# Attention of an encoder layer on one core: two more heads turned by VectorE's blocks and a trip through DRAM, eight weights' low parts by adding transfer, and a new order

## The chip, the core and the metric

The program runs on one core of a Trainium2 chip. The core has TensorE (in the profile PE for matmuls and PEld for weight loads), VectorE (DVE), ScalarE (ACT), GpSimd (POOL) and SyncE (SP, which here only issues transfers). Each engine works through its own queue in order; semaphores hold an instruction until what it needs is there. The metric is the device time of one execution in microseconds (us), here the median of three runs.

## The reference, cut to what matters

One layer for 512 tokens of width 1024, all in float32: a half-step feed-forward network, a mixing stage, a second half-step feed-forward network, a last norm.

```python
x = x + 0.5 * swiglu(rms_norm(x, ffn1_norm), ffn1_w_gate, ffn1_w_up, ffn1_w_down)
h = rms_norm(x, mix_norm)
u = h @ w_in                                   # 1024 -> 512 + 512 + 128 + 128
f_out = fourier_mixer(u[..., :512], fnet_w, fnet_b)
a_out = gqa_attention(u[..., 512:1024], u[..., 1024:1152], u[..., 1152:], q_norm, k_norm)
x = x + jnp.concatenate([f_out, a_out], axis=-1) @ w_out
x = x + 0.5 * swiglu(rms_norm(x, ffn2_norm), ffn2_w_gate, ffn2_w_up, ffn2_w_down)
return rms_norm(x, final_norm)
```

The attention has 8 query heads of 64 channels and 2 key and value heads. For every head the scores are 512 by 512; a softmax runs over the keys; the probabilities then multiply the values.

## The kernel before, in words

Every large matrix product is made of three products of two parts: a value is split into a high part (rounded to the type that the profile calls fp32r) and a low part (the value less its high part). ScalarE makes a high part with a cast, VectorE a low part with a subtraction (`lows`, L204).

The change lies in the mixing stage, lines 850 to 1480. There the program is written as some 630 small named operations, and the string `ORDER` lists their names: each engine gets the instructions of the operations in the order of this list, SyncE's and GpSimd's transfers too. Outside the mixing stage `ORDERS` fixes VectorE's and ScalarE's order; it isn't changed.

The names that are needed:

- `k.0` to `k.7`, `q0.0` to `q3.7`, `v.0` to `v.7`: steps of three matmuls (128 by 512) of the projections. `wq3`, `wv`, `f0` to `f3`, `fw`, `o0` to `o7` are weights of 512 KB (fw half): `.r` loads one into a buffer called raw, `.h` makes its high part (L917), `.l` its low part. There are three raw buffers; one comes free when `.h` and `.l` have read it.
- The four pairs t = 0 to 3 hold the query heads (t, 0) and (t, 1). c counts blocks of 128 queries, kc blocks of 128 keys. `s`tc makes the scores of both heads in two PSUM banks (L1294), `m`tc the negative maxima (VectorE), `e`tbc the exponentials (ScalarE, L1320), which write the tile th of the head, `g`tc the inverse sums, `n`tbc the scaling of th by them (ScalarE, L1356).
- The probabilities must then be turned, so that keys lie along the partitions. For six of the eight heads TensorE does it: `t`tbkc is four transposes of 128 by 128 into a PSUM bank (L1333), `h` and `l` split what it gives (L1338 on ScalarE, L204 on VectorE) into the tiles ph and pl.
- For heads 00 and 01 (`BY_BLOCKS`) it goes otherwise. `T`tbg turns the 32 by 32 blocks of 512 columns in place on VectorE (L1233). `Z`tbg writes these columns, 256 KB, to DRAM (SyncE, L1239). `z`tbg reads 256 KB back into 32 of the 128 partitions of the tile pt (L1246), so that four of them fill pt. `h` (L1260) and `l` split pt.
- `v`tbkc multiplies the values by the two parts (L1367). `o`tb`.c`, `.a` and `r`t bring a pair into place for the output projection.
- `f`hc, `d`, `c`, `map` are the Fourier mixer (L1097 to L1204). `y`d`.0` to `y`d`.7` are the output projection's 64 steps, three matmuls each (L260).

The tiles th and pt have two buffers each: the heads of pair 1 take over the buffers of pair 0.

`ORDER` sets the order of the work and nothing else.

Of the kernel before, what the change touches and what calls it, by code (L numbers as in the profile page):

```python
# [48 lines left out]

ORDERED = {getattr(mybir.EngineType, e) for e in ("PE", "DVE", "Activation", "Pool", "SP")}  # L50
ORDER = """
wk.r wk.h wq0.r wv.r wk.l k.0 k.1 k.2 wq1.r k.3 wq0.h k.4 k.5 k.6 k.7 wq0.l n1.c q0.0 wq2.r cos k.sq wq3.r k.pq q0.1
q0.2 k.sw q0.3 q0.4 n1.m f1.r f2.r q0.5 k.s0 q0.6 k.rc wq1.h wq1.l wq2.h q0.7 k.s1 kw kp q0.sw k.rs q1.0 q1.1 wq2.l
q1.2 km q0.rc q1.3 k.h q1.4 k.l q1.5 q0.sq q0.rs q0.pq q1.6 wv.h q0.s0 q2.0 q0.h q1.7 q0.s1 q0.l wv.l wq3.h s00 q1.sw
m00 s01 s02 m01 q2.1 q2.2 q2.3 q1.sq q1.sd m02 wq3.l e000 q2.4 e010 q2.5 s03 g00 q1.rc e001 q2.6 f0.r e011 q2.7 g01
e002 m03 e012 v.0 q1.pq n000 n011 n001 e013 q3.0 q3.1 q1.rs v.1 e003 g02 f0.h g03 f0.l n010 f3.r n002 q1.s0 n003 v.2
q1.h T002 v.3 q2.sw n013 q1.l T001 T003 q3.2 n012 T013 q3.3 v.4 v.5 q1.s1 n1.p q2.sd q2.sq v.6 q3.4 v.7 Z001 T010 Z003
Z002 q3.5 T000 q3.6 T012 vt s13 s10 Z013 Z012 T011 f1.h q2.rc m13 e103 s11 q3.7 Z000 m11 f1.l m10 q3.sw Z010 q3.sq
e113 f00.0 q2.rs Z011 q3.rc f02.0 f2.h g13 z013 z010 e111 f00.1 f03.0 f2.l vp e101 e110 q3.pq vs z011 e100 z012 s12
h011 h012 v.h m12 v.l z001 l011 h010 f02.1 z003 g10 f00.u e112 q2.pq f01.0 q3.sd e102 l010 f02.e n110 f10.0 n100 v010  # L60
v011 f3.h fw.r g11 z002 z000 n101 f03.1 q2.h q3.rs h013 q2.s0 h000 l012 f12.0 n103 g12 f3.l f01.1 l000 n113 q2.s1 n102
q3.s0 f01.u v012 f03.e h002 o5.r t101 v000 n111 l013 t100 h001 q2.l f10.1 fw.h f03.h f10.u v013 l001 l002 f12.1 v001
h003 v002 q3.h f03.l fw.l l003 f12.e t102 n112 h100 h101 l101 l100 o2.r v003 o01.c o00.c s22 s23 h102 o00.a o01.a v100
l102 v101 pos t103 m22 t110 r0.h f02.h f11.0 h103 m23 f11.1 h110 e212 f12.h f11.u t112 f02.l v102 l103 e213 l110 t113
t111 h112 e203 o0.r v103 q3.l l112 s21 g23 e202 s20 f13.0 o10.c f13.1 n203 m21 h113 e211 o10.a map1 e201 m20 o2.h l113
v110 e200 e210 o2.l d00 map1.h g21 f13.e o1.r map1.l n201 map0 h111 map0.h g22 d01 g20 d10 l111 d11 d0.h n202 d0.l
v111 v112 n200 d1.h f13.h t200 v113 c0.s map0.l f12.l d1.l h200 c1.c f13.l o11.c c0.c c1.s c0.q l200 q3.s1 c0.o t201
n210 o11.a d20 t202 n212 o3.r c1.q h201 d21 h202 c1.o n213 t203 d2.h v200 l201 l202 s33 h203 s32 d2.l n211 v201 l203
c2.s t212 c0.h o0.h m33 m32 d30 d31 e313 t211 h212 c2.q d3.h c0.l e312 v202 h211 l212 c2.c v203 t210 t213 d3.l c2.o
s31 l211 h210 l210 c3.s m31 v210 e302 o0.l c1.h v211 c3.q c1.l s30 m30 o1.h v212 e311 e303 e301 y0.0 c2.h o1.l o6.r  # L70
o4.r g31 g32 e310 h213 e300 l213 c2.l c3.c y0.1 g33 g30 y2.0 n301 n302 n303 y2.1 y1.0 y1.1 v213 r0.l y0.2 y2.2 y1.2
n300 t301 c3.o t300 o20.c t302 o20.a t303 c3.h n311 c3.l y1.3 h300 y0.3 h301 n313 l300 h302 v300 l302 l301 h303 n310
y1.4 y2.3 v301 n312 o21.c t310 o21.a h310 y2.4 t311 l310 t312 v302 t313 r1.h l303 r2.h v303 r1.l h311 v310 l311 v311
h312 h313 o30.c l312 y0.4 l313 v312 o30.a v313 r2.l o31.c y2.5 o31.a y0.5 y2.6 r3.h y1.5 r3.l y1.6 y2.7 o5.h y1.7 y0.6
o5.l y0.7 y0.x y5.0 y5.1 o3.h o7.r y5.2 o3.l y3.0 y2.x y2.h y5.3 y2.q y3.1 y1.x y3.2 y5.4 y3.3 y2.l y5.5 y5.6 o6.h
y5.7 y3.4 o4.h y1.h o4.l y3.5 y3.6 y3.7 y1.q y4.0 o6.l y0.q y5.x y4.1 y6.0 y3.x y6.1 y4.2 y4.3 y0.h o7.h y1.a y5.q
y6.2 y4.4 y4.5 y2.a y6.3 y3.q y4.6 y4.7 o7.l y4.x y5.h y3.a y6.4 y1.l y4.q y0.l y6.5 y4.a y3.h y6.6 y6.7 y5.l y7.0
y7.1 y6.x y7.2 y5.a y6.h y3.l y7.3 y6.l y6.q y7.4 y6.a y7.5 y4.h y7.6 y7.7 y7.x y4.l y7.q y7.a y7.h y7.l
"""


# [54 lines left out]
def asf(ap):  # L136
    return ap.bitcast(F32)
# [19 lines left out]
def encoder(ctx, tc, A, out):  # L157
    nc = tc.nc
# [21 lines left out]
    dp = ctx.enter_context(tc.tile_pool(name="outside", bufs=1, space=bass.MemoryType.DRAM))  # L180
# [584 lines left out]
    n0, n1 = Norm(0), Norm(1)  # L765
# [89 lines left out]
    with tc.tile_pool(name="mix", bufs=1) as mp, tc.tile_pool(name="mixt", bufs=1) as mt:  # L855
# [4 lines left out]
        pos = mp.tile([P, 4 * 258 + 3 * 256], F32R, name="pos")  # L860
# [9 lines left out]
        cos = mp.tile([P, S], F32, name="cos")  # L870
# [31 lines left out]
        raws, ws = {}, {}  # L902

        def weight_ops(name, src, n=KD):
            @op(f"{name}.r")
            def _():
                raws[name] = raw_tile(src, name, n)

            @op(f"{name}.h")
            def _():  # L910
                ws[name] = hi, lo = tuple(weight_slots())
                if name in FURTHER_IN:

# [3 lines left out]
                (nc.vector.tensor_copy if name in HI_DVE else nc.scalar.copy)(hi[:, :n, :], raws[name][:, :n, :])  # L917
# [105 lines left out]
        kw = tp.tile([P, 4, 2, HD], F32, tag="wide", bufs=1, name="kw")  # L1023
# [203 lines left out]
        def block_ops(t, b):  # L1227

            for g in range(4):

                @op(f"T{t}{b}{g}")
                def _(g=g):
                    nc.vector.transpose(heads[t, b][:, g], heads[t, b][:, g])  # L1233

                @op(f"Z{t}{b}{g}")
                def _(g=g):
                    if (t, b) not in outside:
                        outside[t, b] = dp.tile([4, P, S], F32, tag="blocks", bufs=4, name=f"out{t}{b}")
                    nc.sync.dma_start(out=outside[t, b][g], in_=heads[t, b][:, g])  # L1239

                @op(f"z{t}{b}{g}")
                def _(g=g):
                    if (t, b) not in moved:
                        moved[t, b] = mt.tile([P, 4, S], F32, tag="pt", bufs=2, name=f"pt{t}{b}")
                    source = outside[t, b][g].rearrange("(a i) f -> i a f", a=4)
                    nc.sync.dma_start(out=moved[t, b][g * 32 : (g + 1) * 32], in_=source)  # L1246

            def natural(p):
                return p.rearrange("p (c a j) -> p a c j", c=4, a=4)

            for kc in range(4):
                n = f"{t}{b}{kc}"

                def source(kc=kc):
                    return moved[t, b][:, :, kc * P : (kc + 1) * P].rearrange("p a (c j) -> p a c j", c=4)

                @op(f"h{n}")
                def _(n=n, source=source):
                    ph = mt.tile([P, S], F32R, tag="ph", bufs=3, name=f"ph{n}")
                    nc.scalar.copy(natural(ph), source())  # L1260
# [450 lines left out]
```

## Time and profile before

| | |
|---|---|
| time, median of 3 runs (lowest, highest) | 816.61 us (816.13, 816.92) |
| the profiled execution | 816.57 us, of which the span of the profile is 814.8 us |
| PE busy | 806.6 us, 99% |
| DVE busy, ACT busy, POOL busy | 648.6, 498.2, 66.6 us |
| granted TensorE clock | 0.998 |
| the mixing stage's matmuls | 330.22 to 482.77 us |

Times in the profile count from the span's start. A busy engine counts an instruction from its start to its end, overlapped parts once; a mean of one instruction counts them each time. Where the text gives a window such as 400 to 432, it is from a view that lists the busy time of each engine in a stretch.

### The profile page before, as it was taken

How to read it: one execution, taken by the hardware profiler on the slowest of the kernel's cores; microseconds unless marked ns; L12 is line 12 of the kernel's file. 1: busy time of each engine (PE TensorE's matmuls, PEld its weight loads, DVE VectorE, ACT ScalarE, POOL GpSimd, SP SyncE). 2: the span in 40 equal slices, each digit the busy share in tenths (PEclk: the TensorE clock that was granted, in tenths of full speed). 3: DMA queues.
4: the chain of work that ended last, by engine and by line, in shares of the span. 5: the costliest groups of instructions: out<-in, count | busy, mean ns of one | idle time of the engine just before them, and what ended most of it. 6: DMA issues, size and time to landing. Idle time of an engine off the chain costs nothing.

```text
span 814.8 us, 13024 instructions
## 1 busy us (share of the span) xinstructions
PE 806.6 (99%) x4936; PEld 721.5 (89%) x4936; DVE 648.6 (80%) x1065; ACT 498.2 (61%) x864; POOL 66.6 (8%) x75
## 2 busy tenths in 40 slices
PE   9999999999999999999999999999999999999997
PEld 6888998899989998888888888899988998899987
DVE  7997997489956867799998578999955997489674
ACT  7883674267623735687999549557633674267462
POOL 0320000000000000020200003100100000000001
PEclk9999999999999999999999999999999999999999
DMA  7884553345443423339301146554443553345223
GB/s 259 194 178 161 152 137 82 133 130 168 85 139 95 129 72 117 120 111 262 124 27 52 62 123 146 130 188 140 134 118 114 153 140 83 130 130 144 61 78 103
DMA packets 39838, 103.95 MB, mean 128 GB/s; under 512 B 4704, under 2 KB 10976, under 8 KB 39776
## 3 DMA queue, kind: packets, MB, share of 16 engines
q1 hardware_dynamic: 30080, 86.80, 32.9%
q0 software_dynamic: 8832, 15.34, 11.2%
q10 hardware_dynamic: 864, 0.98, 0.4%
q8 instruction: 38, 0.62, 0.3%
q14 instruction: 24, 0.20, 0.1%
HBM read 95.51 MB, written 4.19 MB: 122 GB/s over the span
## 4 chain that ended last, share of the span: by engine, by line
PE 92%; ACT 3%; DVE 3%; issue 1%; DMA 1%; POOL 0%; POOLq 0%; DVEq 0%
PE dn L260 26%; PE r L510 12%; PE r L515 8%; PE gu L260 8%; PE mix L260 6%; PE q L510 4%; PE q L515 4%; PE r L506 4%; PE p L506 4%; PE q L506 4%; PE gu L814 3%; PE p L515 2%; PE mix L1367 2%; PE mix L1333 1%; ACT th L1320 1%
## 5 line engine op out<-in xcount | busy, mean ns | idle before, releaser
L260 PE MATMUL dn<-at,ring 128*128 128x512 f32 x900 | 202.5, 380 | 0.0
L260 PEld LDWEIGHTS dn<-at,ring 128*128 128x128 f32 x900 | 168.0, 188 | 28.7
L515 PE MATMUL r<-rt,ring 128*128 128x256 f32 x560 | 154.3, 276 | 0.0
L510 PE MATMUL r<-rt,ring 128*128 128x256 f32 x840 | 147.0, 276 | 0.0
L510 PEld LDWEIGHTS r<-rt,ring 128*128 128x128 f32 x840 | 127.0, 188 | 1.6
L515 PEld LDWEIGHTS r<-rt,ring 128*128 128x128 f32 x560 | 105.1, 188 | 0.2
L465 ACT CAST ring<-s 128x1024 fp32r<-128x1024 f32 x70 | 73.6, 1051 | 35.5 <-PE r L510 16.5
L204 DVE TENSOR_TENSOR ring<-s,ring 128x1024 fp32r<-128x1024 f32 x70 | 85.2, 1217 | 12.1 <-ACT ring L465 10.2
L649 DVE SCALAR_TENSOR_TENSOR gx<-dn,gx 128x512 f32<-128x512 f32 x61 | 41.9, 688 | 61.8 <-PE dn L260 61.7
L246 ACT CAST ring<-raw_dn 128x768 fp32r<-128x768 f32 (+3 forms) x58 | 45.3, 784 | 71.0 <-PE dn L260 55.2
L515 PE MATMUL q<-rt,ring 128*128 128x256 f32 x280 | 77.0, 275 | 0.0
L234 POOL DMA_DIRECT2D ring<-in_wgu x38 | 32.9, 866 | 469.4 <-ACT u L524 362.5
L204 DVE TENSOR_TENSOR ring<-raw_dn,ring 128x768 fp32r<-128x768 f32 (+3 forms) x58 | 51.5, 891 | 9.6 <-ACT ring L246 5.3
L515 PEld LDWEIGHTS q<-rt,ring 128*128 128x128 f32 x280 | 52.6, 188 | 0.0
L204 DVE TENSOR_TENSOR ring<-raw_g,ring 128x1024 fp32r<-128x1024 f32 x35 | 42.7, 1219 | 9.8 <-PE p L506 9.5
L510 PE MATMUL q<-rt,ring 128*128 128x256 f32 x280 | 49.8, 277 | 0.0
L260 PE MATMUL gu<-ring 128*128 128x512 f32 x216 | 48.9, 381 | 0.0
L506 PE MATMUL r<-rt,ring 128*128 128x512 f32 x140 | 48.7, 384 | 0.0
L506 PE MATMUL p<-rt,ring 128*128 128x512 f32 x140 | 48.3, 382 | 0.0
L506 PE MATMUL q<-rt,ring 128*128 128x512 f32 x140 | 48.3, 382 | 0.0
L260 PEld LDWEIGHTS gu<-ring 128*128 128x128 f32 x216 | 40.4, 188 | 6.9
L465 ACT CAST ring<-raw_g 128x1024 fp32r<-128x1024 f32 x35 | 36.8, 1052 | 14.2 <-DMA raw_g<-in_wgu 11.2
(276 smaller groups left out, 1625.8 us busy)
## 6 DMA issues: line engine op xcount, KB each, us to landing
raw_g<-in_wgu SPq DMA_DIRECT2D x35, 512.0 KB, 3.9
raw_u<-in_wgu SPq DMA_DIRECT2D x35, 512.0 KB, 4.5
raw_dn<-in_wd SPq DMA_DIRECT2D x40, 384.0 KB, 3.2
ring<-in_wgu POOLq DMA_DIRECT2D x35, 256.0 KB, 4.3
raw_gu<-in_wgu SPq DMA_DIRECT2D x12, 512.0 KB, 4.0
raw_o<-in_wo SPq DMA_DIRECT2D x8, 512.0 KB, 3.5
raw_dn<-in_wd SPq DMA_DIRECT2D x8, 448.0 KB, 3.4
raw_wq<-in_wins SPq DMA_DIRECT2D x4, 512.0 KB, 3.3
```

Source lines behind the costliest of these rows:

```text
L204: nc.vector.tensor_tensor(out=lo, in0=src, in1=asf(hi), op=ALU.subtract)
L234: nc.gpsimd.dma_start(out=lo, in_=src, accum_op=ALU.add)
L246: nc.scalar.copy(hi[:, :n, :], raw[:, :n, :])
L260: nc.tensor.matmul(ps, a, b, start=first and b is mhi and a is whi, stop=last and a is wlo)
L465: nc.scalar.copy(hi, src)
L506: nc.tensor.matmul(turned(ps), whi[:, ks], turned(m), start=start, stop=False, skip_group_check=True)
L510: nc.tensor.matmul(ps[:, t], whi[:, ks], m[:, o * HALF :][:, t], start=start and o == 0, stop=False, skip_group_check=True,)
L515: nc.tensor.matmul(o, wlo[:, ks], m, start=False, stop=stop, skip_group_check=True)
L649: nc.vector.scalar_tensor_tensor(out=x[d][:, t], in0=ps[:, t], scalar=0.5, in1=x[d][:, t], op0=ALU.mult, op1=ALU.add)
L814: nc.tensor.matmul(turned(pss[c]), w[:, k % 2, c], turned(m[k]), start=k == 0 and m is hh and w is hi, stop=k == KD - 1 and w is lo,)
L1320: nc.scalar.activation(prob[t, b, c], scores, AF.Exp, bias=mxs[n][:, b : b + 1], scale=f[:, b : b + 1], accum_out=zs[t][:, c, b : b + 1],)
L1367: nc.tensor.matmul(turned(outs[t, b]), w, turned(p), start=kc == 0 and i == 0, stop=kc == 3 and i == 1)
```

## The change

Heads 10 and 11 join `BY_BLOCKS`: their eight operations `t` (four transposes each) go from TensorE, and `T`, `Z`, `z` come in for them. What is written to DRAM gets another layout, so that one `z` of 256 KB now fills a row of 2 KB in each of the 128 partitions of pt, instead of four such rows in each of 32 partitions; still all four `z` of a head are needed before its first `h`.

For the eight weights of `REST_IN`, `.l` is no longer VectorE's subtraction. A new operation `.w` lets ScalarE write the negative of the high part into the low part's place, and `.l` is then a transfer of GpSimd's queue that reads the weight once more from DRAM and adds it there. The raw buffer is free after `.h`.

`ORDER` is written anew.

```diff
-BY_BLOCKS = "00", "01"
-REST_BY_DMA = {'00': (), '01': ()}
+BY_BLOCKS = "00", "01", "10", "11"
+REST_BY_DMA = {'00': (), '01': (), '10': (), '11': ()}
+REST_IN = "wq3", "wv", "f1", "f2", "f3", "o0", "o1", "o2"
...
 ORDER = """
-wk.r wk.h wq0.r wv.r wk.l k.0 k.1 k.2 wq1.r k.3 wq0.h k.4 k.5 k.6 k.7 wq0.l n1.c q0.0 wq2.r cos k.sq wq3.r k.pq q0.1
...
+wq0.r wq1.r wk.r wq2.r cos wk.h wq0.h wk.l k.0 k.1 k.2 k.3 k.4 k.5 k.6 wv.r wq3.r f2.r wq1.h wq0.l n1.c k.7 k.sq q0.0
...
+            if name in REST_IN:
+
+                @op(f"{name}.w")
+                def _():
+                    hi, lo = ws[name]
+                    nc.scalar.activation(lo[:, :n, :], asf(hi[:, :n, :]), AF.Copy, scale=-1.0)
+
+                @op(f"{name}.l")
+                def _():
+                    nc.gpsimd.dma_start(out=ws[name][1][:, :n, :], in_=src, accum_op=ALU.add)
+
+                return
...
                     if (t, b) not in outside:
-                        outside[t, b] = dp.tile([4, P, S], F32, tag="blocks", bufs=4, name=f"out{t}{b}")
-                    nc.sync.dma_start(out=outside[t, b][g], in_=heads[t, b][:, g])
-
-                @op(f"z{t}{b}{g}")
-                def _(g=g):
+                        outside[t, b] = dp.tile([4, 4, 32, S], F32, tag="blocks", bufs=4, name=f"out{t}{b}")
+                    nc.sync.dma_start(out=outside[t, b][:, g], in_=heads[t, b][:, g])
+
+            for a in range(4):
+
+                @op(f"z{t}{b}{a}")
+                def _(a=a):
                     if (t, b) not in moved:
                         moved[t, b] = mt.tile([P, 4, S], F32, tag="pt", bufs=2, name=f"pt{t}{b}")
-                    source = outside[t, b][g].rearrange("(a i) f -> i a f", a=4)
-                    nc.sync.dma_start(out=moved[t, b][g * 32 : (g + 1) * 32], in_=source)
+                    nc.sync.dma_start(out=moved[t, b][:, a], in_=outside[t, b][a].rearrange("g i f -> (g i) f"))
```

Three places of the new order matter below. Line numbers of the new program are some 16 higher in this part.

**ScalarE, where the exponentials of pair 1 begin.** Before, th_3506 and th_3511 are heads 00 and 01 and th_3661 is head 10, which takes the buffer of head 00:

```order
L1016 CAST near<-rot_q_3523 128x512
L954 ACTIVATE own_q_3585<-mix_3295,qkg 128x512
L1356 ACTIVATE th_3511<-th_3511,z_3505 128x4x4x32 x2
L946 ACTIVATE sq_q_3611<-mix_3295 128x512
L1053 COPY vt<-mix_3291 128x512
L1320 ACTIVATE th_3661,z_3660<-mix_3290,mx_3656,sc 128x512
```

Now (th_3493 and th_3495 are heads 00 and 01, th_3679 and th_3690 heads 11 and 10; L926 is a `.w`):

```order
L1372 ACTIVATE th_3495<-th_3495,z_3492 128x4x4x32 x4
L1372 ACTIVATE th_3493<-th_3493,z_3492 128x4x4x32 x4
L969 ACTIVATE own_q_3652<-mix_3288,qkg 128x512
L961 ACTIVATE sq_q_3662<-mix_3292 128x512
L919 CAST more<-raw_f_3337 128x1024
L961 ACTIVATE sq_q_3676<-mix_3288 128x512
L1336 ACTIVATE th_3679,z_3678<-mix_3291,mx_3624,sc 128x4x4x32
L1031 CAST near<-rot_q_3612 128x512
L1068 COPY vt<-mix_3293 128x512
L926 ACTIVATE more<-more 128x1024
L1336 ACTIVATE th_3690,z_3678<-mix_3290,mx_3624,sc 128x4x4x32
```

Head 01 is scaled, turned and written out before head 00; head 11 comes first in pair 1 and takes head 01's buffer, and three other instructions stand between it and head 10's first exponential.

**TensorE, where the first heads meet the values.** Before, the transposes of head 10 (L1333) stand between the products with the values (L1367):

```order
L1367 MATMUL mix_3293<-ph_3772,near 128x4x32x4
L1367 MATMUL mix_3293<-pl_3875,near 128x4x32x4
L1333 MATMUL mix_3290<-ident,th_3661 128x128 x4
L1367 MATMUL mix_3294<-ph_3873,near 128x4x32x4
L1367 MATMUL mix_3294<-pl_3904,near 128x4x32x4
L1333 MATMUL mix_3295<-ident,th_3661 128x128 x4
```

Now there is none in this part (L1310 are scores of pair 2, L1383 the products with the values of head 00):

```order
L1310 MATMUL mix_3294<-ks_3277,near 128x4x32x4
L1310 MATMUL mix_3292<-ks_3277,near 128x4x32x4
L1383 MATMUL mix_3293<-ph_3869,near 128x4x32x4
L1383 MATMUL mix_3293<-pl_3911,near 128x4x32x4
L1383 MATMUL mix_3293<-ph_3872,near 128x4x32x4
L1383 MATMUL mix_3293<-pl_3908,near 128x4x32x4
```

The eight groups of heads 10 and 11 are gone from TensorE's queue; the sixteen groups of pairs 2 and 3 stay.

**SyncE, behind the first two heads.** Before, the weights of the output projection follow the last reads:

```order
L968 DMA sw_q_3682<-own_q_3683 32x512 x4
L228 DMA raw_fw<-in_fw 128x512
L1246 DMA pt_3780<-out_3622 32x4x512 x2
L228 DMA raw_o_3920<-in_wo 128x1024
L228 DMA raw_o_3999<-in_wo 128x1024
```

Now (out_3880 is head 10, out_4008 head 11, pt_4016 and pt_4069 are what is read back of them):

```order
L230 DMA raw_fw<-in_fw 128x512
L1262 DMA pt_3722<-out_3629 128x512 x2
L1254 DMA out_3880<-th_3690 4x32x512 x3
L1254 DMA out_4008<-th_3679 4x32x512 x2
L1254 DMA out_3880<-th_3690 4x32x512
L1254 DMA out_4008<-th_3679 4x32x512 x2
L1262 DMA pt_4016<-out_3880 128x512 x4
L230 DMA raw_o_4066<-in_wo 128x1024
L1262 DMA pt_4069<-out_4008 128x512 x4
L230 DMA raw_o_4074<-in_wo 128x1024
```

Sixteen more transfers stand in this queue, and those into pt_4069 wait until head 01's last low part (`l012`) has been read out of the buffer that pt_4069 takes over.

More of the change, by code (lines that the diff above doesn't have):

```diff
@@ L51 @@
 ORDER = """
-wk.r wk.h wq0.r wv.r wk.l k.0 k.1 k.2 wq1.r k.3 wq0.h k.4 k.5 k.6 k.7 wq0.l n1.c q0.0 wq2.r cos k.sq wq3.r k.pq q0.1
[L53 to L76, printed above, removed]
@@ L77 @@
-y6.2 y4.4 y4.5 y2.a y6.3 y3.q y4.6 y4.7 o7.l y4.x y5.h y3.a y6.4 y1.l y4.q y0.l y6.5 y4.a y3.h y6.6 y6.7 y5.l y7.0
-y7.1 y6.x y7.2 y5.a y6.h y3.l y7.3 y6.l y6.q y7.4 y6.a y7.5 y4.h y7.6 y7.7 y7.x y4.l y7.q y7.a y7.h y7.l
+wq0.r wq1.r wk.r wq2.r cos wk.h wq0.h wk.l k.0 k.1 k.2 k.3 k.4 k.5 k.6 wv.r wq3.r f2.r wq1.h wq0.l n1.c k.7 k.sq q0.0
+q0.1 q0.2 q0.3 k.pq n1.m wq1.l k.rc k.s0 q0.4 q0.5 f1.r pos q0.6 k.s1 q0.7 wq2.h k.sw q1.0 k.rs kw wq2.l q1.1 kp q0.sw
+km q1.2 q1.3 q0.rc q1.4 k.h wv.h q0.sq q0.rs q1.5 k.l q0.h q1.6 q1.7 q0.pq q0.l s01 q1.sq q1.sw q0.s0 wq3.h wv.w wq3.w
@@ new lines @@
+q0.s1 q1.rc s02 s00 q2.0 m01 q2.1 e001 e011 m02 m00 q2.2 e010 e002 e012 q2.3 q2.4 q1.sd q1.rs n1.p wq3.l q2.5 s03 q1.h
+e000 q1.pq q2.6 q2.7 m03 q1.l s12 g02 g00 f1.h g01 q3.0 e013 q2.sw e003 q3.1 q3.2 q3.3 q3.4 q3.5 q3.6 wv.l q3.7 v.0
+v.1 q1.s0 v.2 v.3 f0.r f3.r q1.s1 n010 g03 q2.rc n011 n013 n012 q2.sd v.4 m12 T010 Z010 v.5 T012 v.6 T013 T011 n003
+n002 n001 n000 Z012 Z013 Z011 T000 T002 T001 T003 q3.sw Z002 q2.rs Z001 v.7 q2.sq q3.rc s10 f0.h Z003 Z000 f2.h q3.sq
+e112 q2.h q2.l m10 vt f2.w e102 g12 f0.l e110 e100 q2.pq s11 s13 vp f1.w m11 g10 z012 o6.r z003 z001 z000 q3.sd z002
@@ new lines @@
+n102 e111 e101 m13 f00.0 f1.l f01.0 q3.pq n112 e103 q2.s0 vs e113 h001 q3.s0 g11 q3.rs l001 g13 z011 v.h h000 f02.0
+f03.0 n101 n100 s23 f00.1 f02.1 n103 v.l l000 n113 f00.u n110 q3.h n111 T100 v000 T103 f02.e T102 fw.r z010 z013 h002
+f02.h h003 T113 T111 T112 T101 f2.l q2.s1 Z103 f03.1 f01.1 v001 l003 T110 l002 f11.0 s22 v002 Z100 f01.u f3.h f03.e
+m22 f3.w v003 h013 h011 f12.0 f10.0 h010 fw.h o00.c e202 e212 m23 o00.a g22 e203 e213 s20 q3.s1 f3.l Z102 s21 Z111
+Z112 l010 Z101 Z113 Z110 z103 m20 n202 n212 f03.h m21 l011 e200 e210 h012 g23 l013 g20 l012 v010 e201 f10.1 z102 z101
@@ new lines @@
+z100 f10.u h100 e211 n210 n213 o1.r fw.l z111 z113 z110 z112 o2.r f12.1 v011 f13.0 v012 v013 map0 map1 o01.c h101
+map0.h h103 l100 g21 f02.l f03.l q3.l l101 f12.e f11.1 v100 v101 d00 n211 h102 f12.h h110 map1.h n201 d01 d0.h map0.l
+o01.a l103 d10 f13.1 l110 map1.l l102 v110 v102 f11.u o2.h n200 h111 d0.l v103 f13.e c0.s c0.c d11 t210 f12.l f13.h
+h112 l111 f13.l l112 d20 t211 v111 v112 o10.c c0.q d1.h o10.a c0.o d1.l n203 h113 l113 h210 h211 d21 c0.h c1.s o0.r
+v113 d2.h c1.q o11.c l210 l211 c0.l t201 c1.c t212 t202 v210 o0.h d2.l o11.a c1.o h212 c2.s s33 h201 l212 l201 m33
@@ new lines @@
+o0.w o1.h v211 o0.l h202 c2.q v212 t200 l202 d30 h200 c2.c d31 o1.w l200 d3.h c1.h c2.o t213 t203 v200 h213 v201 v202
+h203 d3.l o4.r o3.r s32 l213 e303 e313 l203 s31 s30 o2.w o1.l v213 m32 e302 e312 o2.l m30 v203 c1.l y0.0 c2.h e300
+e310 c2.l c3.s g33 g30 m31 g32 y0.1 y0.2 y1.0 y1.1 c3.c c3.q r0.h n300 y1.2 r0.l c3.o n303 e311 e301 y2.0 g31 n302
+n301 y2.1 y2.2 c3.h t301 t302 n311 h301 t300 o20.c r1.h h300 h302 n310 n313 o21.c n312 c3.l l301 l300 l302 o20.a r1.l
+y0.3 y2.3 y2.4 y1.3 o21.a t303 y1.4 v300 h303 v301 v302 t310 l303 t311 h310 l310 h311 l311 v303 t312 o30.c h312 t313
@@ new lines @@
+v310 v311 y2.5 l312 h313 l313 v312 r2.h v313 o31.c r2.l o30.a o31.a r3.h y0.4 y0.5 y0.6 y2.6 y1.5 r3.l y2.7 o3.h y0.7
+o6.h y1.6 y1.7 o5.r o7.r o3.l o4.h y3.0 y3.1 y3.2 y1.x o6.l y2.x y3.3 y3.4 y3.5 y3.6 y3.7 y6.0 o5.h y1.q y0.x o4.l
+y3.x o5.l y0.q y2.q y3.q y3.h y2.h y4.0 y6.1 y4.1 y5.0 y5.1 y6.2 y6.3 y6.4 y5.2 y6.5 y6.6 y4.2 y5.3 y5.4 y6.7 y5.5
+y1.a y2.l y2.a y0.h y3.a y3.l o7.h y1.h y6.x o7.l y0.l y5.6 y4.3 y4.4 y4.5 y4.6 y5.7 y4.7 y1.l y5.x y4.x y5.q y6.h
+y5.h y4.h y7.0 y7.1 y7.2 y7.3 y4.q y6.q y7.4 y5.l y4.l y4.a y5.a y6.l y7.5 y7.6 y7.7 y7.x y7.q y6.a y7.h y7.a y7.l
```

## The prediction

> **What bounds the kernel now.** I read the busy times first, then TensorE's waits, then a table of the mixing stage by stretches.
>
> ```profile
> PE 806.6 (99%) x4936; PEld 721.5 (89%) x4936; DVE 648.6 (80%) x1065; ACT 498.2 (61%) x864; POOL 66.6 (8%) x75
> PE mix L1097 <- ACT th L1320: 1.2, 1, 1.2
> PE mix L1333 <- ACT th L1356: 0.3, 1, 0.3
> ```
>
> TensorE is busy 99% of the span at a granted clock of 0.998, and in the mixing stage it stands still only twice, for 1.2 and 0.3 us. So work taken from TensorE shortens the run, as long as nobody else holds it up. Who could do that is in the next view; its columns are the stretch, its length, the busy time of PE, PEld, DVE, ACT and POOL with their instructions, then clock, DMA share and GB/s.
>
> ```profile
> 335.69:366.75 31.06, 31.06 (x159) 25.32 (x158) 27.67 (x51) 27.45 (x47) 6.30 (x4) 1.00 0.35 113
> 366.75:372.17 5.42, 5.17 (x37) 3.90 (x35) 5.32 (x10) 0.00 (x1) 0.00 (x0) 1.00 0.95 347
> 372.17:400.00 27.83, 26.91 (x210) 24.66 (x211) 26.24 (x50) 26.46 (x53) 5.35 (x5) 1.00 0.78 215
> 400.00:432.00 32.00, 31.67 (x225) 26.88 (x223) 30.18 (x63) 30.62 (x64) 0.00 (x0) 1.00 0.05 17
> 432.00:448.77 16.77, 16.77 (x93) 14.29 (x93) 12.98 (x26) 16.02 (x31) 0.00 (x0) 1.00 0.19 64
> 450.31:482.77 32.46, 32.46 (x148) 27.47 (x148) 20.73 (x28) 15.83 (x23) 0.00 (x0) 1.00 0.25 82
> ...
> 335.69 0.60 ACT L946 ACTIVATE sq_k<-mix 128x512 f32<-128x512 f32 x1 [3.31 <-PE mix L260]
> ...
> 447.70 1.07 ACT L1338 CAST ph<-mix 128x512 fp32r<-128x512 f32 x2 [0.28 <-PE mix L1367]
> ```
>
> I call the time from ScalarE's first instruction on the keys (335.69) to its last split of turned probabilities (447.70 + 1.07 = 448.77) the attention stretch. It is 113.08 us long. Over it ScalarE is busy 27.45 + 0 + 26.46 + 30.62 + 16.02 = 100.55 us, so idle 12.53 us; from 372 on it is busy 73.1 of 76.6 us, 95%. The page's 61% is a mean with the feed-forward stages and hides that. After the stretch come the last products with the values and then 49 steps of the output projection in 32.46 us, all TensorE. In the new order too 15 steps of that projection stand ahead of the last product with the values and 49 behind it, so the end of the run moves by what the attention stretch moves. Everything outside it (both feed-forward networks, the closing norm) has the same instructions in the same order on TensorE, and I leave it at zero.
>
> **The change part by part.** *TensorE loses eight groups of four transposes.* The row of the chain of waits and the group's row:
>
> ```profile
> 439.08 1.75 PE mix L1333 x16
> ...
> L1333 PE MATMUL mix<-ident,th 128*128 128x128 f32 x96 | 13.4, 273 | 0.3 <-ACT th L1356 0.3
> ```
>
> Back to back, 16 take 1.75 us, 0.109 each (the 273 ns overlap). 32 fewer: 32 x 0.109 = 3.5 us off TensorE. If nothing else bound the stretch, that and the 1.2 us wait above would be the gain: 4.7 us, the lower end.
>
> *VectorE swaps work.* In come eight block transposes, out go eight subtractions of 128x1024:
>
> ```profile
> 364.17 4.26 DVE L1233 STREAM_TRANSPOSE th<-th 128x512 f32<-128x512 f32 x7
> ...
> L204 DVE TENSOR_TENSOR more<-raw_wq,more 128x1024 fp32r<-128x1024 f32 x2 | 2.5, 1226 | 0.3 <-ACT more L917 0.3
> L1338 ACT CAST ph<-mix 128x512 fp32r<-128x512 f32 x24 | 13.6, 591 | 1.0 <-PE mix L1367 0.5 <-PE mix L1333 0.4
> L1260 ACT CAST ph<-pt 128x512 fp32r<-128x512 f32 x8 | 4.9, 623 | 0.3 <-DMA raw_o<-in_wo 0.3
> ```
>
> 8 x 0.61 in, 8 x 1.23 out: VectorE is relieved by 4.9 us of its 102.4 in the stretch (27.67 + 5.32 + 26.24 + 30.18 + 12.98). It doesn't bind. The splits of heads 10 and 11 stay, from SBUF in place of PSUM: 8 x (0.623 - 0.591) = 0.3 us more on ScalarE, which I drop.
>
> *ScalarE gains eight negations of 128x1024.* The trace has the same operation in the feed-forward stages, and two casts of that size back to back in this one:
>
> ```profile
> L233 ACT ACTIVATE ring<-ring 128x1024 fp32r<-128x1024 f32 x3 | 3.2, 1057 | 0.0
> ...
> 339.10 1.05 ACT L917 CAST more<-raw_wq 128x1024 fp32r<-128x1024 f32 x1
> 340.05 1.04 ACT L917 CAST ring<-raw_wq 128x1024 fp32r<-128x1024 f32 x1
> ```
>
> One occupies 1.06 us alone and starts 0.95 after the one before it in a full queue. All eight stand inside the stretch. Out of it goes one cast (wq1's high part, now ahead of the keys); the other differences cancel. Net 7 x 0.95 = 6.7 us: ScalarE must be busy 100.55 + 6.7 = 107.2 us. To give TensorE its whole gain, the stretch would be 113.1 - 4.7 = 108.4 long and ScalarE idle 1.2 us in it, where it now idles 12.5. **This is the term that decides**: the gain is 12.53 - 6.7 = 5.9 us less the idle time that ScalarE keeps.
>
> *What idle time stays.* 5.42 of the 12.53 is one wait:
>
> ```profile
> ACT th L1320 <- DMA out<-th: 5.4, 1, 5.4
> ACT near L1386 <- DVE oo L1382: 1.0, 1, 1.0
> ACT th L1320 <- DVE mx L1304: 0.5, 1, 0.5
> ACT ph L1338 <- PE mix L1367: 0.5, 2, 0.3
> ...
> DMA to landing us min/median/max: 2.2/2.8/3.3
> L1239 SPq DMA_DIRECT2D out<-th x8: 393/516/637, 366.4 to 370.5; - x8
> ```
>
> The first exponential of pair 1 needs a tile th, and gets it when four writes to DRAM of a head of pair 0 have landed. Before, the freeing head's last write was sixth of the eight in SyncE's queue. Now head 01's four block transposes and writes come first and head 11 takes that buffer: two issues (2 x 0.52 us) and up to four transposes (4 x 0.61) earlier, 3.4 us. The other buffer is wanted after an exponential, a cast, a copy and a negation (about 3 us later), which covers the rest of its writes. I put 1.3 us in place of 5.4. The remaining 7.1 us are many waits of 0.3 to 1.1 on TensorE and VectorE. ScalarE is now later against both, so most of them shrink; a few (the last head's chain) can't. Bounds: nothing, or all 7.1. I take 2.8, nearer the low end, because from 372 to 449 ScalarE idled only 3.5 us even while TensorE set the pace. Idle: 1.3 + 2.8 = 4.1 us. The stretch: 107.2 + 4.1 = 111.3, **1.8 us shorter**.
>
> *GpSimd's and SyncE's transfers.* Eight adding transfers of 512 KB, and for heads 10 and 11 eight writes and eight reads:
>
> ```profile
> ring<-in_wgu POOLq DMA_DIRECT2D x3, 512.0 KB, 5.5
> raw_f<-in_winf SPq DMA_DIRECT2D x4, 512.0 KB, 3.5
> ...
> L1246 SPq DMA_DIRECT2D pt<-out x8: 303/425/592, 371.1 to 380.3; - x8
> DMA to landing us min/median/max: 3.4/4.8/6.5
> ```
>
> A low part came 1.2 us after the high part and now comes 1.0 + 5.5. The tightest is f1: between its negation's turn and the first use of its low part TensorE has four half projections (4 x 1.4), a score block (0.8) and a transposition, 6.8 us, against 5.5. I cost it at nothing; on a DMA at 0.78 busy (372 to 400) a landing of 7 would cost 0.2 to 1 us. For the o weights the DMA is at 0.05 to 0.25, with 10 us of cover.
>
> [...]
>
> **The rivals.**
>
> *The whole gain.* ScalarE's small waits vanish, TensorE stays the bound: 816.6 - 4.7 = 811.9, or about 812.5 with a stop or two. For it: ScalarE's waits after 372 are short. Against it: ScalarE at 99% over 108 us, while score blocks on TensorE wait for PSUM banks that only exponentials free.
>
> *No gain.* ScalarE keeps 5.9 us of idle time, say 1.3 + 4.6, and the TensorE time that the transposes left turns up as waits for exponentials and splits: 816.6. The change then moves work without doing what taking it from the bound engine should do.
>
> *Slower.* The read-back of head 11. Its tile pt takes head 01's buffer, so its first read waits for head 01's last low part. Then come four issues (4 x 0.43), a landing of 4.8, and ScalarE's first split of head 11. Ahead of that split ScalarE has 13 instructions of 0.5 to 0.8 us, about 7.5, against 0.7 + 1.7 + 4.8 = 7.2. At the median it just fits; at the 6.5 of the longest row ScalarE stands 1.4 us, with the maps, the Fourier matrices' high parts and a scaling queued behind it, and TensorE behind those. With that and all 7.1 us of the other waits kept: 107.2 + 1.3 + 7.1 + 1.4 = 117.0 us, 3.9 slower than now at the worst; half of it, 818.5, is my figure. It decides where the four reads take over 5 us, or where ScalarE's small waits don't shrink.
>
> **How the numbers follow.** The profiled execution took 816.57 us (814.8 of span and 1.8 around it), the median of the runs is 816.61: the same. Forecast: 816.6 - 1.8 = 814.8. Chances: forecast (813.6 to 816) 0.42, whole gain 0.18, no gain 0.21, slower 0.19. The forecast's own range comes from an idle time of 2.9 to 5.3 us. The range for 8 in 10 runs from 812.2 to 818.4: it leaves out the last bit of the whole gain and the worst of the slower case. About 0.2% (1.6 us) is what a measurement of this kernel can tell from no change. Faster by more than that: the whole gain and two thirds of the forecast, 0.46; within it: the rest of the forecast and most of "no gain", 0.34; slower: 0.20.
>
> **What would show it.** Right: PE's transposes (L1349 there) at 64, some 3.5 us less TensorE work in the stage; ScalarE 97% busy or so from the first exponential of pair 1 to the last split, with TensorE's waits naming exponentials and splits; the wait of that first exponential for DRAM writes at 1 to 2 us. Wrong: ScalarE idle over 6 us in the stretch; TensorE waiting on GpSimd's transfers into ring or more; a wait of the split of pt for the read-back over 1 us; a change outside the mixing stage.

## The result, and the profile after

The changed kernel takes 857.21 us (median of 4 runs, 856.68 to 857.95) where the kernel before takes 816.37 us in the same session. The ratio is 1.050, with a 95% interval of 1.0482 to 1.0518: 41 us slower. The prediction said 814.8 us, at most 818.4. The profiled execution has a span of 854.9 us, 40.1 more than before.

The page of the changed kernel shows where (busy times, then the span in 40 slices of 21.4 us):

```profile
PE 811.8 (95%) x4904; PEld 722.9 (85%) x4904; DVE 646.1 (76%) x1065; ACT 506.3 (59%) x872; POOL 74.0 (9%) x83
...
PE   9999999999999999948279999999999999999997
...
PEclk9999999999999999978779999999999999999999
```

TensorE is down from 99% to 95%, and all of it is in four slices of the mixing stage; in the same four its clock is granted at 0.7 to 0.8. The waits of TensorE and of ScalarE say on what (total, times, longest):

```profile
PE mix L1310 <- ACT th L1336: 26.5, 3, 15.5
PE mix L1075 <- ACT th L1336: 7.5, 1, 7.5
PE mix L1383 <- DVE pl L206: 0.9, 1, 0.9
...
ACT th L1336 <- DMA out<-th: 32.1, 3, 15.7
ACT th L1336 <- DMA pt<-out: 4.2, 1, 4.2
...
ACT ph L1276 <- DMA pt<-out: 2.6, 1, 2.6
```

Before, the exponentials waited 5.4 us for writes to DRAM and TensorE 1.2 us for exponentials. Now it is 32.1 and 34.0. The chain is: a write is late, so a tile th is late, so an exponential is late, so a bank of PSUM (in the rows a tile mix, which takes the scores) is not freed and TensorE has nothing to write scores into. The stage by stretches (columns as in the prediction: busy time of PE, PEld, DVE, ACT and POOL, then clock, DMA share, GB/s):

```profile
370.00:377.00 7.00, 1.57 (x12) 0.91 (x10) 0.00 (x0) 0.00 (x0) 0.00 (x0) 0.93 0.26 102
...
382.00:387.00 5.00, 0.00 (x0) 0.00 (x0) 0.00 (x0) 0.00 (x0) 0.00 (x0) 0.50 0.26 102
...
418.00:426.00 8.00, 0.00 (x0) 0.00 (x0) 0.00 (x0) 0.00 (x0) 0.00 (x0) 0.50 0.26 99
...
434.00:438.00 4.00, 4.00 (x19) 3.03 (x16) 3.93 (x11) 4.00 (x10) 0.00 (x0) 0.57 0.04 12
...
442.00:487.05 45.05, 44.65 (x280) 38.12 (x279) 38.38 (x76) 44.48 (x85) 2.58 (x3) 1.00 0.36 90
```

From 382 to 387 and from 418 to 426 no engine does anything: the core waits for transfers. And the DMA engines aren't full. Their share, a mean over the sixteen that the page counts, is 0.26, as much as four full engines would give (4 / 16 = 0.25), at some 100 GB/s. In the kernel before the same bytes went at a share of 1.03 and 385 GB/s:

```profile
368.00:370.00 2.00, 2.00 (x18) 1.47 (x15) 2.00 (x4) 0.00 (x0) 0.00 (x0) 1.00 1.03 385
```

Eight writes of 256 KB are 2.1 MB: 5.5 us at 385 GB/s, 20.6 us at 102. The row of the write in the changed kernel, and its chain of waits (start, length, what):

```profile
L1254 SPq DMA_DIRECT2D out<-th x16: 507/1588/4480, 363.2 to 416.9; - x16
...
374.08 13.44 DMA out<-th
...
416.89 14.66 DMA out<-th
```

The last write of each pair of heads lands 13.4 and 14.7 us after its issue, against 2.2 to 3.3 before. Even the issues slow down: 1.59 us at the median, against 0.52. One thing that differs from before is the shape of the write in SyncE's queue: 4x32x512 in place of 128x512.

### The profile page after: what moved, and what is told of

Same layout as the page of the kernel before. It is cut to its first block, busy times and chain, and to the rows that moved or that the text cites. A ratio compares the mean times of both kernels' runs of the same rounds, so it can differ in the third digit from the quotient of the medians.

```text
span 854.9 us, 13013 instructions
## 1 busy us (share of the span) xinstructions
PE 811.8 (95%) x4904; PEld 722.9 (85%) x4904; DVE 646.1 (76%) x1065; ACT 506.3 (59%) x872; POOL 74.0 (9%) x83
## 4 chain that ended last, share of the span: by engine, by line
PE 82%; ACT 5%; DMA 5%; DVE 4%; SPq 1%; issue 1%; POOL 0%; DVEq 0%; POOLq 0%; ACTq 0%
PE dn L262 23%; PE r L512 11%; PE r L517 7%; PE gu L262 7%; PE mix L262 5%; PE q L512 4%; PE q L517 4%; PE r L508 4%; PE q L508 4%; PE p L508 4%; DMA out<-th 3%; PE gu L816 3%; PE p L517 2%; ACT th L1336 1%; ACT th L1372 1%
## 5 line engine op out<-in xcount | busy, mean ns | idle before, releaser
L467 ACT CAST ring<-s 128x1024 fp32r<-128x1024 f32 x70 | 73.6, 1051 | 35.8 <-PE r L512 16.5
```

The source lines that it names most:

```text
L467: nc.scalar.copy(hi, src)
```

## The experiments

The first theory (T1 in the expectations) was that this shape alone causes the loss. Its rivals: the load that more transfers put on the queues (T2), and the new order (T3). Ratios are against the kernel before, measured beside each experiment on the same chip. Each experiment has a short name, e1 to e12.

**e1: the old layout in the changed kernel.** Three lines, back to what they were:

```diff
-outside[t, b] = dp.tile([4, 4, 32, S], F32, ...)
+outside[t, b] = dp.tile([4, P, S], F32, ...)
-nc.sync.dma_start(out=outside[t, b][:, g], in_=heads[t, b][:, g])
+nc.sync.dma_start(out=outside[t, b][g], in_=heads[t, b][:, g])
-nc.sync.dma_start(out=moved[t, b][:, a], in_=outside[t, b][a].rearrange("g i f -> (g i) f"))
+source = outside[t, b][a].rearrange("(a i) f -> i a f", a=4)
+nc.sync.dma_start(out=moved[t, b][a * 32 : (a + 1) * 32], in_=source)
```

> The changed kernel with the old layout in DRAM: a write goes to 128 rows of one stride, a read goes back into 32 partitions. Order, four heads by blocks and adding transfers stay. T1 (the write of 4x32x512 is served by four DMA engines in place of sixteen, and its slow landing is the whole loss): the DMA share during the writes is about 1.0 in place of 0.26, ScalarE's waits for them come to under 8 us in place of 32, TensorE's two long stalls are gone, and the time is 812 to 819 us. T2 (the loss comes from the load that four more adding transfers and two more heads put on the DMA queues) and T3 (the new order is at fault): the stalls stay, and the time is over 840 us.

Measured: 824.5 us, ratio 1.0082 (1.0064 to 1.0100). Of the loss of 5.0% the layout takes 4.2 points. T2 and T3 fall as causes of the large loss; 0.8% remain, more than T1 expected. The writes land as fast as before (the first line below), and none of ScalarE's waits names them any more. TensorE's longest waits now are on the second line, and the chain shows what they hang on:

```profile
DMA to landing us min/median/max: 2.0/2.2/4.0
...
PE mix L1114 <- DMA ring<-in_winf: 4.8, 2, 2.6
...
375.96 8.33 DMA ring<-in_winf
...
393.22 9.40 DMA ring<-in_winf
```

These are adding transfers, of f1's low part and of f3's. They land 8.3 and 9.4 us after their issue, not 5.5.

**e3: the shape alone, in the kernel before.** One row more behind each 32 rows of the DRAM tile, so that the write can't be described as 128 rows of one stride; the read skips that row and keeps its shape, 32x4x512:

```diff
-outside[t, b] = dp.tile([4, P, S], F32, ...)
+outside[t, b] = dp.tile([4, 4, 33, S], F32, ...)
-nc.sync.dma_start(out=outside[t, b][g], in_=heads[t, b][:, g])
+nc.sync.dma_start(out=outside[t, b][g, :, :32], in_=heads[t, b][:, g])
-source = outside[t, b][g].rearrange("(a i) f -> i a f", a=4)
+source = outside[t, b][g, :, :32].rearrange("a i f -> i a f")
```

> The kernel before with one thing changed: the DRAM tile has one row more behind each 32, so that the write of a quarter head has the shape 4x32x512 and not 128x512. Nothing is moved. T1: eight writes of 256 KB go at about 100 GB/s and take some 21 us in place of 5.5, ScalarE's wait of 5.4 us for the first exponential of pair 1 becomes 15 to 22 us, and the time is 827 to 836 us. T2 and T3: within 1.5 us of the kernel before.

Measured: 833.29 us, ratio 1.0195 (1.0178 to 1.0212). From its waits and its stretches:

```profile
PE mix L1097 <- ACT th L1320: 14.7, 1, 14.7
...
ACT th L1320 <- DMA out<-th: 22.1, 2, 18.9
...
378.00:382.00 4.00, 0.00 (x0) 0.00 (x0) 0.00 (x0) 0.00 (x0) 0.00 (x0) 0.50 0.26 102
```

Order, engines and bytes are those of before; the shape alone brings the share of 0.26 and 16 us for two heads. T1 holds.

**e9: eight in place of four.** As e3, with the additional row behind each 16 (the write is 8x16x512); the read of a quarter is issued as two of 16x4x512. The new lines:

```diff
+outside[t, b] = dp.tile([4, 8, 17, S], F32, ...)
+nc.sync.dma_start(out=outside[t, b][g, :, :16], in_=heads[t, b][:, g])
+for u in range(2):
+    source = outside[t, b][g, u:8:2, :16].rearrange("a i f -> i a f")
+    r = g * 32 + u * 16
+    nc.sync.dma_start(out=moved[t, b][r : r + 16], in_=source)
```

> The kernel before, its DRAM tile with one row more behind each 16, so that the write of a quarter head has the shape 8x16x512; the read of a quarter becomes two reads of 16x4x512, so that its outermost dimension stays at 16. T1 (as many DMA engines as the outermost dimension has steps, at most sixteen): the eight writes run on eight engines, at a DMA share near 0.5 and about 195 GB/s, 2 MB in 10 to 11 us, between the 5.5 of 128x512 and the 21 of 4x32x512; ScalarE's wait for the first exponential of pair 1 is 8 to 12 us in place of 5.4 (22.1 with four), and the time is 818 to 823 us. If anything with a third dimension falls to four engines: 830 to 835 us, as with 4x32x512. If the split depends on the padding alone, also 830 or more.

Measured: 825.26 us, ratio 1.0116 (1.0102 to 1.0130), some 2 us above the expected time; the mechanism is as expected:

```profile
ACT th L1322 <- DMA out<-th: 11.1, 1, 11.1
...
374.00:376.00 2.00, 0.00 (x0) 0.00 (x0) 1.73 (x4) 0.00 (x0) 0.00 (x0) 1.00 0.53 205
```

So an outermost dimension of 4, 8 and 128 went with shares of 0.26, 0.53 and 1.03, and 102, 205 and 385 GB/s. Times sixteen the shares are 4.2, 8.5 and 16.5: by estimate four, eight and sixteen engines. Divided by that number, each engine moves 25.5, 25.6 and 24.1 GB/s: nearly the same in all three, as it would be if the engines in use were full and the others idle; no row here shows an engine by itself. The padding alone doesn't explain it, since e3 and e9 both have it.

**e2: is the read held too?** The write of e1, but a read into all 128 partitions, whose source in DRAM is then 4x32x512; the new lines:

```diff
+source = outside[t, b][:, a * 32 : (a + 1) * 32]
+nc.sync.dma_start(out=moved[t, b][:, a], in_=source)
```

> As the experiment with the old layout, but the read goes back into all 128 partitions, from a source of 4x32x512 in DRAM. T1 in its wide form (any transfer whose DRAM side has an outermost dimension of four is served by four engines): the reads run at a share of 0.26, four of them take some 10 us in place of 4.8, ScalarE's waits for pt rise by 5 to 20 us and the time is 822 to 845 us. T1 in its narrow form (only the write is): the time is within 2 us of the old layout's.

Measured: 844.56 us, ratio 1.0332 (1.0315 to 1.0349). The wide form holds: one side of the read has an outermost dimension of four, the other 128 partitions, and from 390 to 394, with reads still under way, the share is 0.26, at 100 GB/s.

```profile
ACT ph L1277 <- DMA pt<-out: 26.0, 3, 13.6
...
390.00:394.00 4.00, 0.00 (x0) 0.00 (x0) 1.38 (x2) 0.45 (x1) 0.00 (x0) 0.66 0.26 100
```

**e7: the new addresses with another shape.** The changed kernel, each write cut into four of 32x512:

```diff
-nc.sync.dma_start(out=outside[t, b][:, g], in_=heads[t, b][:, g])
+for a in range(4):
+    nc.sync.dma_start(out=outside[t, b][a, g], in_=heads[t, b][a * 32 : (a + 1) * 32, g])
```

> The changed kernel with its new layout in DRAM and its reads into 128 partitions as they are; only each write of 4x32x512 is issued as four writes of 32x512, so the same bytes go to the same addresses. T1 (what counts is the outermost dimension of one transfer): the writes run at a DMA share near 1.0, the two long stalls are gone, and the time is 818 to 830 us, since SyncE has 64 issues in place of 16. If the new addresses themselves were slow (rows of one transfer 32 apart in DRAM banks), it stays over 845 us.

Measured: 839.01 us, ratio 1.0283 (1.0269 to 1.0297). This is 18 us below the changed kernel, with the same bytes at the same addresses, so the addresses aren't slow. It is above the expected range, the DMA share is 0.52 and not near 1.0 (374 to 378 us, 132 GB/s), and stalls of up to 5.8 us are left: one write of 64 KB per issue of 0.42 us is all that SyncE sends, and its 64 issues are the largest part of the chain of waits from 335 to 470 us (15%). The transfers themselves land soon:

```profile
L1255 SPq DMA_DIRECT2D out<-th x64: 302/424/1393, 363.7 to 411.8; - x64
...
DMA to landing us min/median/max: 1.6/1.7/4.7
```

**e11: the same shape from another queue.** The changed kernel with `nc.gpsimd.dma_start` in place of `nc.sync.dma_start` for the writes, in a single run.

> The changed kernel with the sixteen writes issued on GpSimd's queue in place of SyncE's; shape 4x32x512 and addresses stay. If the split over four engines belongs to the shape of a transfer, whatever queue issues it: DMA share 0.26 during the writes and 850 us or more. If it belongs to SyncE's way of issuing: share near 1.0, no waits over 8 us for the writes, 820 to 835 us.

Measured: 841.9 us, between the two expectations. The first row is of its stretches, the second is the write's (size, median us to landing):

```profile
374.00:378.00 4.00, 0.00 (x1) 0.00 (x1) 0.00 (x0) 0.92 (x3) 0.00 (x0) 0.54 0.81 185
...
out<-th POOLq DMA_DIRECT2D x16, 256.0 KB, 11.3
```

Each write is still slow (11.3 us), but the share is 0.81, by estimate 13 engines of sixteen, and 185 GB/s are more than the 102 of SyncE's queue: several writes in flight don't seem to share the same four engines there, as by the estimate they do on SyncE's queue (0.26). For that share the rate is low (385 GB/s went with 1.03), which no run here explains.

**e4: the adding transfers alone.** The kernel before, the eight `.l` as negation and adding transfer in the place of VectorE's subtraction (`REST_IN` and the return behind this block left out):

```diff
+            if name in REST_IN:
+
+                @op(f"{name}.l")
+                def _():
+                    hi, lo = ws[name]
+                    rest_by_dma(lo[:, :n, :], hi[:, :n, :], src)
```

> The kernel before with one thing changed: the low parts of the eight weights come by negation on ScalarE and adding transfer, at the places where VectorE's subtractions stood. T1: this has nothing to do with the loss of 41 us; by itself it costs ScalarE eight times 0.95 us and makes the low parts 5.5 to 10 us later, so 0 to 10 us more than before. T2: over 20 us more, with waits of ScalarE on writes of th over 15 us.

Measured: 839.95 us, ratio 1.0278 (1.0264 to 1.0293): 23 us, where 10 at most were expected. That much T2 had expected too, but its other sign, long waits of ScalarE for writes, isn't there, so T2 has no support. TensorE waits for the transfers themselves, which in that order are used soon after:

```profile
PE mix L1109 <- DMA ring<-in_winf: 10.0, 2, 7.2
PE mix L261 <- DMA ring<-in_wo: 3.2, 2, 2.3
PE mix L261 <- DMA more<-in_wins: 2.1, 1, 2.1
```

**e5 and e6: what is left of 0.8%.** Both have e1's layout. In e5 `REST_IN` is empty, in e6 f1, f2 and f3 are taken out of it; the names `.l` (VectorE's subtraction again) stand where `.w` stood, and right behind `.h` for f1 (and for wv, wq3 and o2 in e5), so that the raw buffers come free in time.

> The changed kernel with the old layout in DRAM and without any adding transfer: the low parts of the eight weights are VectorE's subtractions again, each right behind its high part or in the place of its negation. New order and four heads by blocks stay. Theory A (what the old layout leaves over the kernel before, 7 us, is the adding transfers' landing: TensorE stood still 9.9 us for two landings of 8.3 and 9.4 us): these waits vanish and the time is 812 to 817 us. Theory B (the new order or the two more heads cost it): 820 to 826 us, as with the adding transfers.

> As the one without adding transfers, but only the three Fourier weights f1, f2 and f3 go back to subtraction; wq3, wv and the three output weights keep their adding transfers. Theory A, with all of it at the Fourier weights: 813 to 818 us, within 1.5 us of the kernel without any adding transfer. If the other five cost something too, this one stands 2 us or more above that. Theory B: 820 to 826 us.

Measured: e5 829.11 us, ratio 1.0158 (1.0145 to 1.0172); e6 822.42 us, ratio 1.0080 (1.0066 to 1.0094). Theory A falls: e5 lies above both ranges, with VectorE's subtractions now among TensorE's waits, and e6 no longer has the 4.8 us of waits for f's transfers, but 3.4 us of waits for VectorE in their place, and its ratio is e1's. For the other five weights adding transfers are worth 0.8% in this order, presumably since VectorE is relieved. In e6 ScalarE looked like the bound from 402 on, though TensorE is busy without a break in the same rows:

```profile
402.00:410.00 8.00, 8.00 (x59) 7.52 (x58) 6.93 (x15) 7.93 (x18) 0.00 (x0) 1.00 0.51 125
410.00:420.00 10.00, 10.00 (x72) 9.28 (x71) 9.91 (x20) 9.95 (x20) 0.00 (x0) 1.00 0.38 117
420.00:430.00 10.00, 10.00 (x69) 8.66 (x68) 9.83 (x21) 9.93 (x18) 1.10 (x2) 1.00 0.34 75
430.00:440.00 10.00, 10.00 (x53) 7.39 (x52) 8.68 (x21) 10.00 (x22) 1.51 (x2) 1.00 0.90 188
```

**e12: e6 with the five negations on GpSimd.**

```diff
-nc.scalar.activation(lo[:, :n, :], asf(hi[:, :n, :]), AF.Copy, scale=-1.0)
+nc.gpsimd.tensor_scalar(out=lo[:, :n, :], in0=asf(hi[:, :n, :]), scalar1=-1.0, scalar2=None, op0=ALU.mult)
```

> The kernel with the old layout and f1 to f3 by subtraction (822.4 us), with one thing changed: the five negations that are left (wq3, wv, o0, o1, o2) are GpSimd's instead of ScalarE's. In that kernel ScalarE was busy 37.8 of 38 us from 402 to 440, three of the negations among them. Theory S (from there on ScalarE's work sets the pace, as the prediction had it): three negations of 0.95 us less bring 819 to 820.5 us, and ScalarE's busy share in that stretch falls little. Theory W (waits of one engine on another, which move but stay, set it): 821.8 to 823. If a negation takes GpSimd more than 4 us, the rope's powers behind the first two, or the output weights behind the last three, come late, and the time is over 824.

Measured: 826.58 us, ratio 1.0131 (1.0113 to 1.0149), slower than e6. No theory expected that: over 824 us was expected only for a negation of more than 4 us. A negation takes GpSimd 3.0 us, and ScalarE, relieved, waits instead:

```profile
350.00:366.00 16.00, 14.32 (x64) 10.51 (x61) 12.35 (x27) 11.38 (x24) 8.93 (x6) 0.89 0.62 151
...
430.00:440.00 10.00, 9.32 (x58) 6.88 (x57) 9.64 (x18) 6.48 (x16) 8.40 (x6) 1.00 0.61 129
```

Theory S finds no support: less work on ScalarE didn't shorten anything. But the run doesn't refute it cleanly, since the first two negations also hold up small operations of the rotary embedding behind them in GpSimd's queue (350 to 366).

**e8: four heads by blocks alone.** The kernel before with heads 10 and 11 in `BY_BLOCKS`, the old layout and no adding transfer. In `ORDER` the new names T, Z and z of pair 1 stand where its `t` stood; the splits of pair 1 come later, `s22`, `s23`, `m22`, `m23`, `e212` and `e213` earlier; some names near them move too.

> The kernel before with heads 10 and 11 turned by blocks too, in the old layout, and nothing else of the change: no adding transfer, the old order but for the piece from the transpositions of pair 1 to the Fourier mixer, where the new operations stand and the splits of pair 1 come some 8 us later, behind two score blocks of pair 2 that come earlier. Theory C (two more heads by blocks are worth TensorE's 3.5 us where order and landing allow, and what the change lost beside the layout is the adding transfers and ScalarE's negations): 812 to 816 us. Theory D (the trip through DRAM costs ScalarE and TensorE more waiting than the transpositions cost, whatever the rest): 818 to 828 us, with waits of the splits for pt or of the exponentials for the writes of 3 us or more.

Measured: 824.85 us, ratio 1.0116 (1.0099 to 1.0133), as theory D had it in size. Its waits and two stretches:

```profile
ACT th L1321 <- DVE mx L1305: 6.9, 4, 3.7
ACT th L1321 <- DMA out<-th: 5.0, 1, 5.0
...
390.00:395.00 5.00, 4.36 (x29) 3.34 (x29) 5.00 (x9) 3.78 (x8) 0.45 (x1) 1.00 1.04 390
395.00:400.00 5.00, 4.64 (x34) 3.68 (x32) 4.90 (x11) 2.45 (x5) 0.00 (x0) 1.00 1.05 237
```

The wait for the writes is no longer than before (5.4 us there). The largest wait isn't for the trip but for the maxima that VectorE makes: with eight block transpositions more it is busy 9.9 of 10 us here, and ScalarE 6.2. This order was made by hand and another might do better, so the run shows one price of the two heads, not the least.

**e10: the wait of 5.4 us in the kernel before.** Six names of `ORDER` change places (the sequences below leave out what stands between them), so that head 00's `T` and `Z` stand ahead of head 01's:

```diff
-T002 T001 T003 T013 T010 T000 T012 T011 | Z001 Z003 Z002 Z013 Z012 Z000 Z010 Z011
+T002 T001 T003 T000 T013 T010 T012 T011 | Z001 Z003 Z002 Z000 Z013 Z012 Z010 Z011
```

> The kernel before with six names changed places: head 00's four block transpositions and writes stand before head 01's, since the first exponential of pair 1 needs head 00's buffer. If that wait of ScalarE (5.4 us) is what TensorE's only 1.2 us of idle time hangs on, the wait falls to about 4, TensorE's idle time goes and the time is 815.0 to 815.8 us where the kernel before has 816.4. If ScalarE's later work is what sets the pace, no change: within 0.5 us.

Measured: 815.98 us, ratio 1.0000 (0.9991 to 1.0009). No change, though ScalarE's wait for the writes fell from 5.4 us to 0.7 and TensorE's 1.2 us to 0.3:

```profile
PE mix L1097 <- ACT th L1320: 0.3, 1, 0.3
...
ACT th L1320 <- DVE mx L1304: 5.0, 2, 4.6
...
ACT th L1320 <- DMA out<-th: 0.7, 1, 0.7
```

An exponential waits 4.6 us for VectorE's maxima instead. No version here beats the kernel before.

## Why the prediction was wrong

**The step that failed** is the idle time that ScalarE keeps, in it the sentence "I put 1.3 us in place of 5.4". It takes the landing of a write from the row of the kernel before (2.2, 2.8, 3.3 us), where the shape was 128x512, and counts only the order of issues and transpositions. The order's rows showed the new shape, 4x32x512, and the diff the new tile; that the shape could set the speed was not asked. In its place the runs showed 13.4 and 14.7 us of landing, 32.1 us of waits, and 16 us from this shape alone in the kernel before (e3). The 1.3 doesn't follow from the prediction's own numbers either: 5.4 less 3.4 is 2.0, which would have made the forecast 815.5. The prediction takes the landing of the read too (4.8 us) from a row of the old shape.

What the traces show on shape is the DMA share: 0.26 with an outermost dimension of four, 0.53 with eight, 1.03 with 128, and 0.26 in e2, where one side alone has four. That the share counts engines in use is an estimate from these numbers. The share of 0.81 in e11 suggests that the queue matters as well; which engines served a write, no trace here shows.

**The sum, term by term.** *TensorE's transposes:* 64 are left, as said, but the 3.5 us that this should take off TensorE's work don't show in its busy time (see the open question below). *ScalarE's work:* forecast 107.2 us in the attention stretch, measured 107.72. *Its idle time:* forecast 4.1, measured 43.7 of a stretch of 151.4 us (335.63 to 487.05). With the old layout (e1) the stretch is 118.0 us, 108.0 busy and 10.0 idle: even without the failed step the forecast of 111.3 would have been 6.7 us short. Here the premise "most of them shrink" failed: none of ScalarE's waits in e1 is for writes, so the 10.0 are all other waits, above the prediction's upper bound of 7.1 for them. *After the stalls,* from 442 to 487, ScalarE is busy 44.48 of 45.05 us, the 97% and more that the prediction wanted to see, but only there. *Outside the stage* I had put zero; the span grew 40.1 us and the stretch 38.3, so 1.8 us are elsewhere.

**Adding transfers at nothing** was too low: the cover of 6.8 us stood against landings of 8.3 and 9.4 us in e1, and in an order without cover (e4) they cost 23 us. Yet e6, without f's transfers, gained nothing, so in the changed order going back to subtractions would not have saved the time.

**The slower rival** had the sign and not the mechanism: it priced the read-back of head 11 at 2 us. In the changed kernel the writes ahead of it were late, and the wait of the splits for the read-back was 2.6 us. On where a transposition belongs the runs go only so far: none with four heads by blocks was as fast as the kernel before (the best, e6, took 1.0080 of its time), and e8 shows VectorE full (9.9 of 10 us), but the kernel before itself turns two heads by blocks, and no run takes those back. Nor does a run settle whether a read into 128 partitions is faster: such reads land at a median of 4.8 us in e7, those into 32 partitions at 4.8 in the kernel before and at 6.1 in e1, each beside other traffic. In the changed kernel the layout that allows such a read slowed the write (13.4 and 14.7 us to landing, against 2.2 to 3.3).

**The idle time as a separate term** was a poor model besides. It supposes that a wait taken away is time gained. e10 cut one wait by 4.7 us and gained nothing; e12 took some 4.4 us of work from ScalarE (104.8 to 100.4 in the stretch) and its idle time rose from 12.1 to 20.0.

**What stays open** is the 0.8% of e1 and e6: with the right layout, is it the trip of two more heads or the new order? Replacing f's adding transfers by subtractions doesn't remove it (e6). The runs don't separate the other two, since e8 has a third order. What the rows do show is where it lies. The first is the mixing stage of the kernel before, the second that of e6, both from the first to the last of its matmuls:

```profile
330.22:482.77 152.55, 151.05 (x896) 128.47 (x895) 127.82 (x230) 119.13 (x220) 11.65 (x9) 1.00 0.35 109
...
329.83:486.41 156.58, 151.58 (x864) 126.10 (x863) 127.51 (x232) 123.94 (x225) 16.06 (x14) 1.00 0.55 153
```

TensorE executes 32 transposes less and yet is busy for as long, and it is idle for 5.0 us in place of 1.5. So the 3.5 us of relief turned up neither as time nor as less busy time. The 64 transposes left are busy for 8.6 us where the 96 were for 13.4, but the 96 score matmuls for 15.5 (a mean of 415 ns) where they were for 13.2 (401 ns). So the likely reading is that the others ran less densely; no run shows why.

## What to carry to other kernels

When a change touches the layout of a transfer, read its shape in the queue, both sides, and look for the outermost dimension: with four or eight steps there the DMA share stopped at 0.26 and 0.53 here, where 128 reached 1.03 (by estimate twelve and eight of sixteen engines idle), and such a share with nothing else running is the sign. Take the duration of an operation from a row of the same shape, or treat it as unknown with a wide upper bound. A wait in a list is worth only what the next wait behind it leaves: in e10 4.7 us less of one gave nothing.

## What the runs showed of the hardware

TensorE's clock fell in the long stalls (0.50 from 382 to 387 and from 418 to 426 in the changed kernel) and came back late. In e3 TensorE stood still from about 372 to 386.6; its granted clock was 1.00 from 370 to 374, 0.60 from 374 to 378 and 0.50 from 378 to 382. These rows are of stretches of 1 us behind that:

```profile
387.00:388.00 1.00, 1.00 (x6) 1.00 (x6) 0.69 (x1) 0.62 (x2) 0.00 (x0) 0.50 0.28 107
...
390.00:391.00 1.00, 1.00 (x6) 1.00 (x6) 0.00 (x0) 0.18 (x1) 0.00 (x0) 0.50 0.51 180
391.00:392.00 1.00, 1.00 (x7) 1.00 (x6) 0.17 (x1) 1.00 (x3) 0.00 (x0) 0.55 0.33 64
392.00:393.00 1.00, 1.00 (x11) 1.00 (x10) 0.34 (x1) 1.00 (x2) 0.00 (x0) 1.00 0.92 295
```

For some 5 us after it starts again it runs at a granted clock of 0.50, with 6 or 7 matmuls in a microsecond in place of 11: by estimate about 2.5 us lost (5 us at half the clock). The span of e3 is 17.5 us longer than before (832.3 against 814.8) with 13.5 us more waiting on exponentials (14.7 against 1.2); these 2.5 us would be part of the 4.0 us between the two. So by this estimate the stall of 14.7 us in e3 cost more than its length. And where SyncE's transfers were slow, its issues were slow too: 1.59 us at the median for one write in the changed kernel, up to 4.48, against 0.52 and at most 0.64 before; 0.59 for one read in e2, up to 5.30, against 0.43 and at most 0.59 before.
